# One decoder layer on one core: the 32-row substitution through memory, spatial products in place, q scaled on VectorE

## The chip, the cores and the metric

One Trainium2 chip, one of its cores. The time is device microseconds for one execution of the whole program; the kernel before took 2677.02 us (median of three runs, 2673.93 to 2677.5).

## The reference, cut to what matters

One layer of a hybrid decoder. A group of 2048 new tokens and 8 sample tokens with a stored state share all weights; the width is 1024. One wide input projection feeds branch A (spatial gating in chunks of 128 positions) and branch B (gated DeltaNet with 8 heads of 128, a short convolution on q, k, v); two more projections, merge gates and an output projection follow.

```python
vn = rmsnorm(v, norm_g)
vc = vp.reshape(bsz, n, lc, A_GROUPS, A_GROUP_DIM)
ws = jnp.where(causal, w_s[:, :lc, :lc], 0)
mixed = jnp.einsum('gts,bnsgc->bntgc', ws, vc) + bias
...
t_mat = jnp.where(strict, beta[..., :, None] * kk * decay, 0.0) + jnp.eye(c)
sol = lax.linalg.triangular_solve(t_mat, rhs, left_side=True, lower=True, unit_diagonal=True)
...
q_dec = q * jnp.exp(gc)[..., None]
def step(s, xs):
    v_new = u_c - jnp.einsum('bhck,bhkv->bhcv', w_c, s)
    o_c = jnp.einsum('bhck,bhkv->bhcv', qd_c, s) + jnp.einsum('bhij,bhjv->bhiv', a_c, v_new)
    s = s * gl_c[..., None, None] + jnp.einsum('bhck,bhcv->bhkv', kd_c, v_new)
    return s, o_c
```

The change touches three things of this: the mixing of branch A (`mixed`), the inverse of the unit triangular matrix `t_mat`, and the decay factor on q. The kernel works in chunks of 128.

## The kernel before, in words

**Two halves.** The work is done for f = 0 (1024 tokens) and f = 1 (1032: the other tokens and the 8 samples). In each half a long stream of products runs on TensorE: for every 128 columns of a weight, `products` (line 167) makes 8 x 3 matmuls for each block of tokens, 512 columns wide in the first half and 344 in the second. The three passes are high part by high part, low by high, and high by low of both operands in a rounded type. `load` (line 134) brings a weight block of 512 KB into `raw`, which has one buffer; `split` makes its `hi` on ScalarE (line 147) and its `lo` in two halves on VectorE (line 153), each with two buffers.

**What runs between.** After every STRIDE = 2800 columns of the stream, `step` advances four queues of generators by one `yield` each: the chains (`chq`), the samples (`smq`), the convolutions (`cvq`) and the rest (`bgq`: normalised rows, `v_mix`, then the eight heads in turn). Whatever a generator emits up to its next `yield` is put between the matmuls of the stream at that place; TensorE runs its matmuls in the order written, and the framework orders the other engines' instructions. All DMAs are issued from one queue, SP's, in order.

**v_mix** (line 381) does the mixing of branch A once in each half. `vts` are eight tiles, one for each group, 128 positions by 8 chunks by 128 channels. Each is scaled by the reciprocal norm `rv` on POOL (line 416), multiplied on TensorE by the masked spatial weights `wst` (mx), and VectorE writes `mo` = mx times gain plus bias (line 424), which is stored (line 426) in two pieces of 256 KB a group.

**head** (line 431) prepares one of the eight heads. From pk, the products of k with k and q, VectorE makes the strict triangle `M` and the attention `AT` for eight chunks (lines 500, 501). q is scaled by the decay `G` on POOL (line 503). Then the inverse of the unit triangle begins with the four 32x32 blocks on each chunk's diagonal: all 8 x 4 blocks at once, partition 32q+i holding row i of block q. For each of 31 columns VectorE spreads a row to all partitions of its block with a shuffle (`bc`, line 517), multiplies it by a column of `Yc` (line 518) and subtracts (line 519). `Xc` is the transpose of `Yc`. `Y` and `X` get the blocks (ScalarE line 541, POOL line 544), and the matmuls g1, p2, g2 and p3 join the blocks to 64 and to 128.

```python
        for l in range(31):
            bc = sp.tile([P, 8, 32], F32, tag="bc", name="bc", bufs=2)
            nc.vector.stream_shuffle(bc[:, :, l + 1:], Uc[:, :, l + 1:], [l] * 32)
            nc.vector.tensor_tensor(tmp[:, :, l + 1:], bc[:, :, l + 1:], Yc[:, :, l:l + 1].to_broadcast([P, 8, 31 - l]), ALU.mult)
            nc.vector.tensor_tensor(Yc[:, :, l + 1:], Yc[:, :, l + 1:], tmp[:, :, l + 1:], ALU.subtract)
```

**chain** (line 580) runs the recurrence over a head's eight chunks while the next head is prepared. In each chunk TensorE's p goes to VectorE's r (line 591), r to pz, pz to ScalarE's w (line 597), w to pu, and VectorE's S (line 602) to the next p. After four chunks the output O is normalised (rko, by the helper in lines 93 to 98), scaled (OS, line 614), turned (otr) and written to yT (line 621). **conv** (line 650) makes the short convolution: one product and three product-sums of 128x1024 (line 659) for each of q, k and v of a head.

Tiles with a tag have as many buffers as the tag says; AT has two, the other large tags of a head ("E", "G", "M", "Y", "NV") one.

Of the kernel before, what the change touches and what calls it, by code (L numbers as in the profile page):

```python
# [28 lines left out]
def hybrid_step(tc, d):  # L29
    nc = tc.nc  # L30
    if PIN:
        mm = lambda *a, **k: tc.keep_in_program_order(nc.tensor.matmul(*a, **k))  # L32
# [26 lines left out]
    idc = cst[:, 4 * P + 16:4 * P + 48]  # L59
# [231 lines left out]
    def btile(tag, dt=F32, shape=(P, 8, P)):  # L291
        return sp.tile(list(shape), dt, tag=tag, name=tag, bufs=2 if tag == "AT" else 1)
# [89 lines left out]
    def v_mix(f, vts, ssv, sv):  # L382
# [27 lines left out]
        for g in range(8):  # L410
            wst = sp.tile([P, P], F32, tag="r", name="wst", bufs=2)
            dma(wst, d["ws"][g])
            nc.gpsimd.affine_select(wst, wst, [[1, P]], ALU.is_ge, 0.0, base=0, channel_multiplier=-1)
            bb = sp.tile([P, P], F32, tag="w", name="bb", bufs=2)
            dma(bb, d["bs"][g:g + 1, :].partition_broadcast(P))
            nc.gpsimd.tensor_tensor(vts[g], vts[g], rv.unsqueeze(2).to_broadcast([P, 8, P]), ALU.mult)
            for _ in range(7 if g == 0 else 1):
                yield
            for gi in range(2):
                mx = pg.tile([P, 512], F32, tag="o" if gi == 0 else "kq", name="mx")  # L420
                for n in range(4):
                    mm(mx[:, n * P:(n + 1) * P], vts[g][:, gi * 4 + n, :], wst, start=True, stop=True)
                mo = sp.tile([P, 512], F32, tag="yT", name="mo", bufs=2)
                nc.vector.scalar_tensor_tensor(mo.rearrange("p (n t) -> p n t", t=P), mx.rearrange("p (n t) -> p n t", t=P), gmlpg[:, g:g + 1],
                                               bb.unsqueeze(1).to_broadcast([P, 4, P]), ALU.mult, ALU.add)
                dma(m_sp[f][g][:, gi * 512:(gi + 1) * 512], mo)
                yield


    def head(f, h, T):  # L430
# [84 lines left out]
        for l in range(31):
            bc = sp.tile([P, 8, 32], F32, tag="bc", name="bc", bufs=2)
            nc.vector.stream_shuffle(bc[:, :, l + 1:], Uc[:, :, l + 1:], [l] * 32)  # L517
            nc.vector.tensor_tensor(tmp[:, :, l + 1:], bc[:, :, l + 1:], Yc[:, :, l:l + 1].to_broadcast([P, 8, 31 - l]), ALU.mult)  # L518
            nc.vector.tensor_tensor(Yc[:, :, l + 1:], Yc[:, :, l + 1:], tmp[:, :, l + 1:], ALU.subtract)  # L519
            if (l + 1) * 28 // 31 > l * 28 // 31:  # L520
                yield
        Xc = btile("Xc", shape=(P, 8, 32))
# [9 lines left out]
        NV = btile("NV")  # L532
        for gi in range(2):
            tr = turned(T["v"], "tr", gi)
            for n in range(4):
                c = gi * 4 + n
                nc.scalar.activation(NV[:, c, :], tr[:, tk(n)], AF.Copy, scale=nk[:, c:c + 1])
            if gi == 0:
                for q in range(4):
                    r = slice(32 * q, 32 * q + 32)  # L540
                    nc.scalar.activation(Y[r, :, r], Yc[r], AF.Copy)
                for q in range(2):
                    r = slice(32 * q, 32 * q + 32)
                    nc.gpsimd.tensor_copy(X[r, :, r], Xc[r])
            yield
        g1 = {a: pg.tile([P, 8, 32], F32, tag=t, name="g1") for a, t in ((0, "kq"), (64, "tr"))}
# [15 lines left out]
        nc.gpsimd.tensor_copy(X[32:64, :, 0:32], yt)  # L562
# [170 lines left out]
    def samples():  # L733
# [61 lines left out]
        for h in range(NH):  # L795
# [88 lines left out]
    def v_phase(A, vt_tile, st):  # L884
        spans = [(0, 1), (1, 2), (2, 4), (4, 6), (6, 8)]
        tags = [("Y", 1), ("NV", 1), ("KD", 2), ("KD", 2), ("craw", 2), ("craw", 2), ("AT", 2), ("vT", 1)]
# [31 lines left out]
        def begin():  # L918
# [347 lines left out]
```

## Time and profile before

| | |
|---|---|
| runs | 2677.5, 2673.93, 2677.02 us; median 2677.02 |
| profiled execution | 2677.51 us, span of the trace 2675.7 us |
| mean granted TensorE clock | 0.991 |
| TensorE busy | 2592.4 us, 97% |
| VectorE, ScalarE, POOL busy | 1552.0, 1048.0, 416.5 us |
| moved by DMA | 280.38 MB, mean 105 GB/s |

The span runs from the first to the last instruction of the trace; the profiled execution has 1.8 us around it. Busy times say how full an engine is, not who holds up whom: for that one looks at what an engine waited for. A released wait is written X <- Y: X could begin when Y had ended. In the page's rows a group of instructions has its line, its engine, what it writes and reads, its count, and then busy time and the mean duration of one in ns.

### The profile page before, as it was taken

The page shows a single profiled execution, that of the slowest core. Times are in us where ns is not written, and L with a number is a line of the kernel's source. Part 1 is how long each engine was busy: PE and PEld are TensorE (multiplying, and loading weights), DVE is VectorE, ACT ScalarE, POOL GpSimd, SP SyncE. Part 2 cuts the span into 40 slices and gives each one's busy share as a digit, 9 for nine tenths or more (in the row PEclk, how much of TensorE's full clock was granted, in tenths as well). Part 3 has the DMA queues.
Part 4 walks back from the last instruction along what each step waited for, and adds up shares of the span by engine and source line. Part 5 has one row for each costly group of instructions (what it writes and reads, how often), then busy time and mean ns, then how long its engine had stood idle before and what let it go on. Part 6 is the DMA issues. An engine that isn't in the chain of part 4 may idle for free.

```text
span 2675.7 us, 42486 instructions
## 1 busy us (share of the span) xinstructions
PE 2592.4 (97%) x15755; PEld 2306.2 (86%) x15755; DVE 1552.0 (58%) x5018; ACT 1048.0 (39%) x2732; POOL 416.5 (16%) x536
## 2 busy tenths in 40 slices
PE   7989999999999999999999999999999999999998
PEld 6778787877878888989999999999989888999886
DVE  6266766765865725256677568467484543442455
ACT  5324453453453423423534534435442332332122
POOL 2021121121211102022111212211111102102000
PEclk9989999999999999999999999999999999999999
DMA  6232212211212214123122121121145876645443
GB/s 207 80 118 68 68 40 75 87 44 60 72 48 72 87 64 131 41 69 119 56 62 64 49 84 57 44 77 61 60 123 185 274 243 238 236 170 182 135 141 102
DMA packets 139792, 280.38 MB, mean 105 GB/s; under 512 B 19944, under 2 KB 75688, under 8 KB 139584
## 3 DMA queue, kind: packets, MB, share of 16 engines
q1 hardware_dynamic: 139584, 277.66, 31.7%
q8 instruction: 124, 2.03, 0.3%
q14 instruction: 84, 0.69, 0.1%
HBM read 205.06 MB, written 72.55 MB: 104 GB/s over the span
## 4 chain that ended last, share of the span: by engine, by line
PE 81%; DVE 11%; DMA 4%; ACT 2%; issue 1%; POOL 0%; SPq 0%; ACTq 0%; DVEq 0%; POOLq 0%
PE acc L167 67%; PE acc L947 2%; PE p L32 2%; PE O L32 2%; DVE vT L659 2%; PE trn L33 2%; DMA xt<-in_x_tok 1%; PE pu L32 1%; PE g L32 1%; PE pz L32 1%; PE pk L32 1%; DVE lo L153 1%; DVE bc L517 1%; DMA m<-mo 1%; DVE nwt L96 1%
## 5 line engine op out<-in xcount | busy, mean ns | idle before, releaser
L167 PE MATMUL acc<-Ah,hi 128*128 128x344 f32 (+1 forms) x3360 | 1200.8, 357 | 2.9 <-ACT Ah L209 2.9
L167 PE MATMUL acc<-Al,hi 128*128 128x344 f32 (+1 forms) x3360 | 1197.5, 356 | 0.4
L167 PE MATMUL acc<-Ah,lo 128*128 128x344 f32 (+1 forms) x3344 | 1193.5, 357 | 0.3 <-DVE lo L153 0.3
L167 PEld LDWEIGHTS acc<-Ah,hi 128*128 128x128 f32 x3360 | 634.6, 189 | 59.6 <-ACT Ah L209 4.1
L167 PEld LDWEIGHTS acc<-Al,hi 128*128 128x128 f32 x3360 | 634.8, 189 | 57.1 <-DVE Al L210 1.0
L167 PEld LDWEIGHTS acc<-Ah,lo 128*128 128x128 f32 x3344 | 633.3, 189 | 55.5 <-issue 0.7
L153 DVE TENSOR_TENSOR lo<-raw,hi 128x512 fp32r<-128x512 f32 x368 | 265.2, 741 | 314.3 <-ACT hi L147 301.8
L147 ACT ACTIVATE hi<-raw 128x1024 fp32r<-128x1024 f32 x185 | 195.6, 1057 | 316.9 <-PE acc L167 283.9
L519 DVE TENSOR_TENSOR Yc<-Yc,tmp 128x248 f32<-128x248 f32 (+30 forms) x496 | 149.0, 300 | 10.0
L517 DVE STREAM_SHUFFLE bc<-Uc 128x248 f32<-128x248 f32 (+30 forms) x496 | 151.5, 310 | 0.0
L518 DVE TENSOR_TENSOR tmp<-bc,Yc 128x248 f32<-128x248 f32 (+30 forms) x496 | 146.0, 294 | 0.5
L487 POOL TENSOR_TENSOR kl<-kq,kh 128x256 fp32r<-128x256 f32 x128 | 99.2, 784 | 237.2 <-ACT kh L486 237.0
L659 DVE SCALAR_TENSOR_TENSOR kq<-craw,convw,kq 128x1024 f32<-128x1024 f32 x96 | 122.8, 1279 | 1.2
L591 DVE SCALAR_TENSOR_TENSOR r<-p,neg,NV 128x128 f32<-128x128 f32 x128 | 44.3, 346 | 129.8 <-PE p L32 129.4
L597 ACT ACTIVATE w<-pz,s_bb 128x128 f32<-128x128 f32 x128 | 47.0, 368 | 174.6 <-PE pz L32 174.3
L167 PE MATMUL acc<-Bh,hi 128*128 128x344 f32 (+1 forms) x320 | 111.9, 350 | 0.0
L167 PE MATMUL acc<-Bh,lo 128*128 128x344 f32 (+1 forms) x320 | 111.9, 350 | 0.0
L167 PE MATMUL acc<-Bl,hi 128*128 128x344 f32 (+1 forms) x320 | 111.6, 349 | 0.0
L1115 POOL TENSOR_TENSOR g<-g,u 128x344 f32<-128x344 f32 (+1 forms) x40 | 45.1, 1128 | 337.3 <-DVE g L1114 337.3
L643 ACT ACTIVATE craw<-acc 128x344 f32<-128x344 f32 (+1 forms) x120 | 61.2, 510 | 92.9 <-PE acc L167 92.5
L452 ACT ACTIVATE junk<-trn 128x128 f32<-128x128 f32 x256 | 67.7, 284 | 42.1 <-PE trn L33 42.1
L1114 DVE TENSOR_TENSOR g<-g,acc 128x344 f32<-128x344 f32 (+1 forms) x40 | 23.3, 582 | 100.4 <-PE acc L167 82.3
(333 smaller groups left out, 3448.3 us busy)
## 6 DMA issues: line engine op xcount, KB each, us to landing
raw<-in_w_blk SPq DMA_DIRECT2D x136, 512.0 KB, 3.7
g<-big SPq DMA_DIRECT2D x16, 516.0 KB, 2.9
g<-g SPq DMA_DIRECT2D x16, 516.0 KB, 5.1
xt<-in_x_tok SPq DMA_DIRECT2D x16, 512.0 KB, 4.7
m<-mo SPq DMA_DIRECT2D x32, 256.0 KB, 2.7
G<-gc SPq DMA_DIRECT2D x16, 512.0 KB, 8.9
g<-big SPq DMA_DIRECT2D x16, 512.0 KB, 2.9
yb<-yT SPq DMA_DIRECT2D x32, 256.0 KB, 2.3
```

The lines of the kernel that those rows point to most:

```text
L32: mm = lambda *a, **k: tc.keep_in_program_order(nc.tensor.matmul(*a, **k))
L33: transpose = lambda *a, **k: tc.keep_in_program_order(nc.tensor.transpose(*a, **k))
L147: nc.scalar.activation(j.hi[:, :, :m], j.raw[:, :, :m], AF.Copy)
L153: nc.vector.tensor_tensor(j.lo[:, p, :m], j.raw[:, p, :m], j.hi[:, p, :m].bitcast(F32), ALU.subtract)
L167: nc.tensor.matmul(out, wt[:, k, :m], at[:, k, off:off + w], start=(i == 0), stop=(i == len(passes) * KB - 1))
L452: nc.scalar.activation(junk, tr[:, tk(n)], AF.Square, accum_out=acc[:, c:c + 1])
L487: nc.gpsimd.tensor_tensor(kl, kq[:, :, tk(c)], kh.bitcast(F32), ALU.subtract)
L517: nc.vector.stream_shuffle(bc[:, :, l + 1:], Uc[:, :, l + 1:], [l] * 32)
L518: nc.vector.tensor_tensor(tmp[:, :, l + 1:], bc[:, :, l + 1:], Yc[:, :, l:l + 1].to_broadcast([P, 8, 31 - l]), ALU.mult)
L519: nc.vector.tensor_tensor(Yc[:, :, l + 1:], Yc[:, :, l + 1:], tmp[:, :, l + 1:], ALU.subtract)
L643: nc.scalar.activation(raw[:, 3 + off:3 + off + w], ps[:, :w], AF.Copy)
L659: nc.vector.scalar_tensor_tensor(acc, raw[:, i:i + HALF], convw[:, blk, i:i + 1], acc, ALU.mult, ALU.add)
```

## The change

1. **v_mix.** The scaling goes from POOL to ScalarE, eight activations of 128x128 for each group, written in place. VectorE writes its product over the scaled input instead of into `mo`, and one store of 512 KB replaces two of 256 KB. `wst` and the bias are fetched two groups ahead, and the scaling of group g+1 is issued behind the first mx of group g.
2. **Substitution.** The 32 rows of a block are spread differently: four blocks q of eight chunks n are 32 blocks; a group of four partitions holds one block, and partition g of it every fourth row. `M`'s diagonal blocks are written to memory (`u_sp`, four DMAs) and read back four times, so that each partition has a whole block (`UB`). Then a column needs no shuffle: two VectorE operations on k x w elements with k = l//4 + 1 and w = 31 - l. The result `YB` goes to memory (`y_sp`, one DMA) and comes back in the old layout as `Yc` in 16 DMAs, in pieces of 128 bytes. The start value is a constant `idy`.
3. **q** is scaled by `G` on VectorE in place of POOL. The copies into `X` go from POOL to ScalarE.
4. **Order.** `Xc` and the copies into `Y` and `X` come later, three yields after the turned v; the generators have new yields. "Y" and "NV" get a second buffer, and the head waits for the end of the previous chain but one (`len(chq) > 1`) and for its own v. `UB` uses the tag "E", so the samples' work, which takes that tag after the last head, may begin only after the last substitution. A memory reserve of POOL is set to 1024 bytes.

```diff
-        for g in range(8):
+        def fetch(g):
             wst = sp.tile([P, P], F32, tag="r", name="wst", bufs=2)
             dma(wst, d["ws"][g])
-            nc.gpsimd.affine_select(wst, wst, [[1, P]], ALU.is_ge, 0.0, base=0, channel_multiplier=-1)
             bb = sp.tile([P, P], F32, tag="w", name="bb", bufs=2)
             dma(bb, d["bs"][g:g + 1, :].partition_broadcast(P))
-            nc.gpsimd.tensor_tensor(vts[g], vts[g], rv.unsqueeze(2).to_broadcast([P, 8, P]), ALU.mult)
-            for _ in range(7 if g == 0 else 1):
+            return wst, bb
+
+        def scaled(g, wst):
+            nc.gpsimd.affine_select(wst, wst, [[1, P]], ALU.is_ge, 0.0, base=0, channel_multiplier=-1)
+            for n in range(8):
+                nc.scalar.activation(vts[g][:, n, :], vts[g][:, n, :], AF.Copy, scale=rv[:, n:n + 1])
+
+        ahead = [fetch(0), fetch(1)]
+        for _ in range(4):
+            yield
+        scaled(0, ahead[0][0])
+        for _ in range(3):
+            yield
+        for g in range(8):
+            wst, bb = ahead.pop(0)
+            for gi in range(2):
+                part = vts[g][:, gi * 4:gi * 4 + 4, :]
+                mx = pg.tile([P, 4, P], F32, tag="o" if gi == 0 else "kq", name="mx")
+                for n in range(4):
+                    mm(mx[:, n, :], part[:, n, :], wst, start=True, stop=True)
+                if gi == 0 and g < 7:
+                    scaled(g + 1, ahead[0][0])
+                nc.vector.scalar_tensor_tensor(part, mx, gmlpg[:, g:g + 1], bb.unsqueeze(1).to_broadcast([P, 4, P]), ALU.mult, ALU.add)
                 yield
...
+            dma(m_sp[f][g][:, 0:HALF], vts[g].rearrange("p n t -> p (n t)"))
+            if g < 6:
+                ahead.append(fetch(g + 2))
+            yield
...
-        nc.gpsimd.tensor_tensor(qT, qT, flat(G), ALU.mult)
+        nc.vector.tensor_tensor(qT, qT, flat(G), ALU.mult)
+        yield from wait(1)
+        for q in range(4):
+            r = slice(32 * q, 32 * q + 32)
+            dma(u_sp[f][h][q].rearrange("n i c -> i n c"), M[r, :, r])
+        UB = sp.tile([P, 32, 32], F32, tag="E", name="UB")
+        yield from wait(1)
+        for q in range(4):
+            dma(UB[32 * q:32 * q + 32], u_sp[f][h].rearrange("q n i c -> (q n) i c"))
+        YB = btile("Uc", shape=(P, 8, 32))
+        nc.scalar.activation(YB, idy, AF.Copy)
+        tmp = btile("tmp", shape=(P, 8, 32))
+        yield from wait(4)
+        for l in range(31):
+            k, w = l // 4 + 1, 31 - l
+            nc.vector.tensor_tensor(tmp[:, :k, l + 1:], YB[:, :k, l:l + 1].to_broadcast([P, k, w]), UB[:, l:l + 1, l + 1:].to_broadcast([P, k, w]), ALU.mult)
+            nc.vector.tensor_tensor(YB[:, :k, l + 1:], YB[:, :k, l + 1:], tmp[:, :k, l + 1:], ALU.subtract)
+            if l % 3 == 3 - 1:
+                yield
...
+        dma(y_sp[f][h].rearrange("g q n k c -> (g q n) k c"), YB)
         Yc = btile("Yc", shape=(P, 8, 32))
+        yield
         for q in range(4):
...
+            for g in range(4):
+                dma(Yc[32 * q + g:32 * q + 32:4], y_sp[f][h][g, q].rearrange("n k c -> k n c"))
+        while len(chq) > 1 or not T.get("v_made"):
+            yield
+        Y, NV = btile("Y"), btile("NV")
...
+        yield from wait(3)
+        Xc = btile("Xc", shape=(P, 8, 32))
+        nc.vector.transpose(Xc, Yc)
```

Three places show what moves. The first is VectorE in the first half, where the substitution of a head meets the chain of the head before it (r and S; `Uc` is the tag in which the new `YB` lies). Before:

```order
625 L591 SCALAR_TENSOR_TENSOR r<-p_3768,neg,NV 128x128
626 L518 TENSOR_TENSOR tmp<-bc,Yc 128x8x28
627 L517 STREAM_SHUFFLE bc<-Uc 128x8x27
628 L519 TENSOR_TENSOR Yc<-Yc,tmp 128x8x28
629 L153 TENSOR_TENSOR lo<-raw,hi 128x512
630 L518 TENSOR_TENSOR tmp<-bc,Yc 128x8x27
631 L517 STREAM_SHUFFLE bc<-Uc 128x8x26
632 L519 TENSOR_TENSOR Yc<-Yc,tmp 128x8x27
633 L517 STREAM_SHUFFLE bc<-Uc 128x8x25
634 L518 TENSOR_TENSOR tmp<-bc,Yc 128x8x26
635 L602 SCALAR_TENSOR_TENSOR S<-S,s_eg,pu 128x128
```

The chain's r and S stand between a substitution's columns. And of the kernel changed, the same place, VectorE:

```order
565 L634 SCALAR_TENSOR_TENSOR S<-S,s_eg,pu 128x128
566 L623 SCALAR_TENSOR_TENSOR r<-p_3725,neg,NV 128x128
567 L634 SCALAR_TENSOR_TENSOR S<-S,s_eg,pu 128x128
568 L623 SCALAR_TENSOR_TENSOR r<-p_3754,neg,NV 128x128
569 L153 TENSOR_TENSOR lo<-raw,hi 128x512 x2
570 L634 SCALAR_TENSOR_TENSOR S<-S,s_eg,pu 128x128
571 L542 TENSOR_TENSOR tmp<-Uc,UB 128x31
572 L543 TENSOR_TENSOR Uc<-Uc,tmp 128x31
573 L542 TENSOR_TENSOR tmp<-Uc,UB 128x30
574 L543 TENSOR_TENSOR Uc<-Uc,tmp 128x30
```

The chain's last S now stands ahead of the first column; the shuffles are gone, and a column's two operations begin with 31 elements on each partition.

The second place is VectorE ahead of a head's g1, in the kernel changed: `Xc`, `yt` and what stands around them.

```order
488 L688 TENSOR_SCALAR kq<-craw,convw 128x1024
489 L153 TENSOR_TENSOR lo<-raw,hi 128x512
490 L691 SCALAR_TENSOR_TENSOR kq<-craw,convw,kq 128x1024 x3
491 L623 SCALAR_TENSOR_TENSOR r<-p_3231,neg,NV 128x128
492 L570 STREAM_TRANSPOSE Xc<-Yc 128x256
493 L688 TENSOR_SCALAR kq<-craw,convw 128x1024
494 L691 SCALAR_TENSOR_TENSOR kq<-craw,convw,kq 128x1024 x2
495 L593 STREAM_TRANSPOSE yt<-Y 32x256
```

`Xc` stood directly behind the substitution's last column before; it now stands among the convolution's operations and one r of the chain.

The third is SP's queue in the kernel changed, from the weight loads during a substitution to those behind it.

```order
69 L135 DMA raw<-in_w_blk 128x1024 x3
70 L549 DMA y_0_185<-Uc 128x256
71 L554 DMA Yc<-y_0_185 8x8x32 x16
72 L135 DMA raw<-in_w_blk 128x1024 x2
73 L719 DMA big<-m_1_90 128x1024
```

The store of the result and its sixteen reads stand between weight loads, where only weight loads stood before.

## Rows read from the trace of the kernel before

**Rows 1.** The page: busy time by engine; costliest groups (busy us, mean ns).

```profile
PE 2592.4 (97%) x15755; PEld 2306.2 (86%) x15755; DVE 1552.0 (58%) x5018; ACT 1048.0 (39%) x2732; POOL 416.5 (16%) x536
...
L517 DVE STREAM_SHUFFLE bc<-Uc 128x248 f32<-128x248 f32 (+30 forms) x496 | 151.5, 310 | 0.0
L518 DVE TENSOR_TENSOR tmp<-bc,Yc 128x248 f32<-128x248 f32 (+30 forms) x496 | 146.0, 294 | 0.5
```

**Rows 2.** PE's waits: line, released by, us in total, times, longest.

```profile
PE pz L32 <- DVE r L591: 13.0, 10, 2.9
PE mx L32 <- DVE mo L424: 10.7, 4, 6.6
...
PE p L32 <- DVE S L602: 9.7, 8, 2.1
PE mx L32 <- DVE rx L98: 8.5, 1, 8.5
PE pk L32 <- DVE yT L621: 3.6, 4, 1.1
```

**Rows 3.** Timeline, 134 to 153 us: start, duration, engine, line, operation.

```profile
134.23 1.90 POOL L416 TENSOR_TENSOR AT<-AT,rv 128x1024 f32<-128x1024 f32 x1
134.33 1.82 DVE L93 TENSOR_SCALAR nwt<-ssx 128x9 int32<-128x9 int32 x1
...
134.60 1.05 PE L32 MATMUL mx<-wst,E 128*128 128x128 f32 x8
...
143.60 0.17 DVE L96 TENSOR_TENSOR nwt<-rx 128x9 f32<-128x9 f32 x1
...
146.70 2.04 PE L32 MATMUL mx<-wst,G 128*128 128x128 f32 x8 [8.47 <-DVE rx L98]
...
150.67 1.73 PE L32 MATMUL mx<-wst,G 128*128 128x128 f32 x8
```

**Rows 4.** Busy us (x instructions) of PE, PEld, DVE, ACT, POOL; PEclk; DMA; GB/s.

```profile
134.00:152.00 18.00, 9.53 (x43) 8.10 (x42) 17.66 (x21) 2.72 (x4) 10.67 (x9) 0.72 0.13 37
...
1165.00:1192.00 27.00, 20.36 (x129) 20.10 (x128) 24.84 (x36) 5.08 (x8) 15.37 (x11) 0.90 0.16 46
```

**Rows 5.** Timeline, 400 to 407 us, in which a substitution begins.

```profile
400.92 0.40 PE L167 MATMUL acc<-Ah,lo 128*128 128x512 f32 x1
...
401.15 0.40 PE L167 MATMUL acc<-Ah,hi 128*128 128x512 f32 x1
...
401.71 0.40 DVE L518 TENSOR_TENSOR tmp<-bc,Yc 128x248 f32<-128x248 f32 x1
...
402.15 0.42 DVE L519 TENSOR_TENSOR Yc<-Yc,tmp 128x248 f32<-128x248 f32 x1
...
406.02 0.49 PE L32 MATMUL pz<-r,Y 128*128 128x128 f32 x2 [2.40 <-DVE r L591]
```

**Rows 6.** Groups by line and shape on VectorE and ScalarE.

```profile
L659 DVE SCALAR_TENSOR_TENSOR kq<-craw,convw,kq 128x1024 f32<-128x1024 f32 x96 | 122.8, 1279 | 1.2
...
L518 DVE TENSOR_TENSOR tmp<-bc,Yc 128x48 f32<-128x48 f32 x16 | 3.3, 206 | 0.0
...
L537 ACT ACTIVATE NV<-trn,s_nk 128x128 f32<-128x128 f32 x128 | 36.5, 369 | 36.8 <-PE trn L33 36.7
```

**Rows 7.** DMA issues: count, KB each, median us from issue to landing.

```profile
m<-mo SPq DMA_DIRECT2D x32, 256.0 KB, 2.7
...
Ss<-in_st_gdn SPq DMA_DIRECT2D x16, 512.0 KB, 4.2
...
wst<-in_ws SPq DMA_DIRECT2D x16, 64.0 KB, 4.0
...
m<-ms SPq DMA_DIRECT2D x8, 4.0 KB, 1.5
```

**Rows 8.** Lines 147 and 135, 300 to 330 us: count, duration, first and last.

```profile
L147 ACT ACTIVATE hi<-raw x2: 1062/1065/1068, 305.3 to 323.3; 128x1024 fp32r<-128x1024 f32 x2
...
L135 SPq DMA_DIRECT2D raw<-in_w_blk x2: 332/332/333, 313.3 to 327.2; - x2
...
DMA to landing us min/median/max: 3.7/3.7/3.7
```

More of the change, by code (lines that the diff above doesn't have):

```diff
@@ L291, in btile @@
     def btile(tag, dt=F32, shape=(P, 8, P)):
-        return sp.tile(list(shape), dt, tag=tag, name=tag, bufs=2 if tag == "AT" else 1)
+        return sp.tile(list(shape), dt, tag=tag, name=tag, bufs=2 if tag in ("AT", "Y", "NV") else 1)
     BT = ["E", "G", "M", "AT", "Y", "NV"]
@@ L409, in v_mix @@
             yield
-        for g in range(8):
+        def fetch(g):
             wst = sp.tile([P, P], F32, tag="r", name="wst", bufs=2)
             dma(wst, d["ws"][g])
-            nc.gpsimd.affine_select(wst, wst, [[1, P]], ALU.is_ge, 0.0, base=0, channel_multiplier=-1)
             bb = sp.tile([P, P], F32, tag="w", name="bb", bufs=2)
             dma(bb, d["bs"][g:g + 1, :].partition_broadcast(P))
-            nc.gpsimd.tensor_tensor(vts[g], vts[g], rv.unsqueeze(2).to_broadcast([P, 8, P]), ALU.mult)
-            for _ in range(7 if g == 0 else 1):
-                yield
[L419 to L427, printed above, removed]
@@ L430, in head, with wait @@
+    u_sp = [[dp.tile([4, 8, 32, 32], F32, name=f"u{f}_{h}") for h in range(NH)] for f in range(2)]
+    y_sp = [[dp.tile([4, 4, 8, 8, 32], F32, name=f"y{f}_{h}") for h in range(NH)] for f in range(2)]
+    def wait(n):
+        for _ in range(n):
+            yield
     def head(f, h, T):
@@ L515, in head @@
[L515 to L522, printed above, removed]
@@ L531, in head @@
         nc.gpsimd.memset(X, 0.0)
-        NV = btile("NV")
         for gi in range(2):
@@ L537, in head @@
                 nc.scalar.activation(NV[:, c, :], tr[:, tk(n)], AF.Copy, scale=nk[:, c:c + 1])
[L538 to L544, printed above, removed]
-            yield
+            yield
+        yield from wait(3)
+        Xc = btile("Xc", shape=(P, 8, 32))
+        nc.vector.transpose(Xc, Yc)
+        for q in range(4):
+            r = slice(32 * q, 32 * q + 32)
+            nc.scalar.activation(Y[r, :, r], Yc[r], AF.Copy)
+        for q in range(2):
+            r = slice(32 * q, 32 * q + 32)
+            nc.scalar.activation(X[r, :, r], Xc[r], AF.Copy)
+        yield from wait(2)
         g1 = {a: pg.tile([P, 8, 32], F32, tag=t, name="g1") for a, t in ((0, "kq"), (64, "tr"))}
@@ L661, in conv @@
             nc.scalar.activation(acc, acc, AF.Silu)
+            if kind == 2:
+                T["v_made"] = True
             if after:
@@ L885, in v_phase @@
         spans = [(0, 1), (1, 2), (2, 4), (4, 6), (6, 8)]
-        tags = [("Y", 1), ("NV", 1), ("KD", 2), ("KD", 2), ("craw", 2), ("craw", 2), ("AT", 2), ("vT", 1)]
+        tags = [("Y", 2), ("NV", 2), ("KD", 2), ("KD", 2), ("craw", 2), ("craw", 2), ("AT", 2), ("vT", 1)]
         def x_tile(i):
@@ L933, in begin @@
             dma(convw, d["convw"])
+            dma(idy, d["idy"])
             dma(abraw, d["w_ab"])
@@ L1229 @@
         np.where(idx[:, None] <= idx[None, :], f4(0), f4(-1e30)).astype(f4),
-        fold, np.tile(np.eye(32, dtype=f4), (4, 1)),
+        fold,
     ], axis=1)
```

22 lines of the change are left out of this document (7 added, 15 removed).

## The prediction, made before any run of the changed kernel

> **What bounds the kernel now.** I read the busy table first: TensorE (PE) is busy 2592.4 of 2675.7 us, VectorE 1552.0, POOL 416.5 [rows 1]. So only what lets PE stand or slows its clock can change the time, and its idle sum is 2675.7 − 2592.4 = 83 us. The list of PE's waits says who owns it [rows 2]: the largest end on VectorE results, pz<-r 13.0 us in 10 waits, mx<-mo 10.7 in 4, p<-S 9.7 in 8, mx<-rx 8.5 in one, pk<-yT 3.6 in 4, 45.5 in all. The other 37.5 are the start of the program and many short gaps.
>
> Then I looked where these waits lie. **The stall in v_mix** is one place. From 134 us POOL runs the 128x1024 scalings of L416, 1.90 us each, and VectorE's tiny 128x9 operations between them take 1.82 us each; as soon as POOL is through, the same kind takes 0.17 [rows 3]. PE stands 8.47 us, since a matmul mx waits behind these operations. [...] The second half has the same pattern, weaker, at 1165 to 1192 us, with a clock of 0.90 [rows 4].
>
> **The start of a substitution** is the other place. At 401.71 us VectorE begins a product of 0.40 us, at 402.15 a difference of 0.42 [rows 5], and a shuffle goes with each pair; the chain's r of the head before lies behind several of them, and PE waits 2.40 us at pz until 406.02 [rows 5].
>
> **Gains.** (1) In v_mix the 16 scalings of 1.90 us on POOL become 128 on ScalarE, 128x128 in place. The nearest row, 128x128 with a scale, is 0.37 us [rows 6], 2.95 us a group. Without POOL's long operations VectorE's small ones fall to the 0.17 us of rows 3, and mx<-mo and mx<-rx go: 10.7 + 8.5 = 19.2 us [rows 2]. Some of mx<-mo is a wait for the store that still reads mo, which lands in 2.7 us [rows 7]; in-place writes take it away too. With the stall goes half clock: (2.04 − 1.05) + (1.73 − 1.05) = 1.7 us on mx alone, L167 between them besides, and at most (1 − 0.90) × 27 = 2.7 in the second half. I take 4 for both.
>
> (2) The substitution loses its 496 shuffles and most of its elements. Before, (151.5 + 2 × 146.0)/16 = 28 us of VectorE a head, taking L519 like L518 [rows 1]. After, 62 operations of 50 elements on average; a 128x48 row is 206 ns [rows 6]. I add 34 ns for the dependence of each on the one before (0.44 from the start of the product to that of the difference, for a duration of 0.40 [rows 5]): 62 × 0.24 = 15 us. A first column takes two operations of 0.2 instead of three of 0.4, and in the built order the chain's r and S stand ahead of the substitution (the first place above). So I take 11 of the 13.0 us of pz<-r, and the 3.6 of pk<-yT, since yT stood in the same crowd [rows 2].
>
> [...]
>
> Sum of gains: 19.2 + 4 + 11 + 3.6 = 37.8 us.
>
> **Costs.** (3) The way through memory must end before g1. By rows: u 4 × 0.33 of issue [rows 8] and a landing of 2.7 (m<-mo); UB 4 × 0.33 + 4.2 (512 KB, Ss); substitution 15 and some four lo in it, 3; y 0.3 + 2.7; Yc 16 × 0.33 + 4.0 (wst, the slowest small one) [rows 7]; Xc about 0.4, like the other 256-element operations: 40 us. In the built order 183 to 207 matmuls of L167 stand on PE between a head's last pk and its first g1 in the first half; at 0.23 us (400.92 to 401.15 [rows 5]) 42 to 48 us, and in the second half 264 to 298 of 344 columns, as much. With the chain's matmuls between I take 47: some 7 us of slack, so nothing for the way itself. But Xc stands behind convolution operations of 1.28 us on VectorE [rows 6] (the second place above), and g1 behind it. Bounds: 0, and two such operations each time, 2.56 × 16 = 41. Nearest is p<-S, which also stands behind them and cost 9.7 in all [rows 2]: half of it, 5.
>
> (4) The q scaling on VectorE. No row has a product of two 128x1024 tensors there; with an addition in it, it is 1.28 us [rows 6], so the 16 cost 0 to 20 us. They stand in front of an M or an S now and then; pk alternates between two PSUM tags. I take 2, against a POOL that is freed.
>
> (5) SP's queue gets 25 more issues a head. It is in order: 16 Yc wait for y to land and hold the weight loads behind them (the third place), 2.7 + 16 × 0.33 = 8 us. The cover: a load issued at 313.3 landed 3.7 us later, and its hi began at 323.3, when the block before had ended, 6 us after; and hi is itself made a block of 18 us ahead of its use (305.3 and 323.3) [rows 8]. So nothing. If that cover were gone, 8 × 16 = 128.
>
> (6) ScalarE has to scale a group, 2.95 us, within three steps. A step is 2800 columns, 5.5 matmuls, 1.3 us, and two of the three carry an mx of 1.05 [rows 3]: 6 us, but a hi of 1.06 [rows 8] and copies can stand ahead. Bounds 0 and 2 × 14 = 28; I take 2.
>
> (7) The samples' work, which waits for the last substitution, comes nearer to the half's boundary: 0 to a landing of 4.2 [rows 7]; I take 1.
>
> Costs: 5 + 2 + 2 + 1 = 10. Net −27.8 against the profiled 2677.51 us (span 2675.7, 1.8 around it), which is the highest of the three runs, 0.5 above their median 2677.02: **2650 us**.
>
> **Rivals.** *A: VectorE stays as crowded at the wrong moments.* 62 short operations, a q scaling and Xc put as much in front of r, S and M as now, and only v_mix pays: 19.2 + 4 − 10 = 13, 2664 us. For it: p<-S comes from convolutions, which stay. Against it: at 401 us it is the columns of the substitution that r waits behind.
>
> *B, slower: the way through memory is late at g1.* u and Yc move pieces of 128 bytes. If each of the four landings takes 3 us more than the rows I used (5.7 for 2.7, 7.2 for 4.2), the way is 12 us longer, 5 to 6 beyond the slack, and PE stands 16 × 6 = 96 us: 2650 + 96 = 2746. It decides from 9 us on: 2 beyond the slack, 2 × 16 = 32, eats the gain. Against it: m<-ms landed in 1.5 us [rows 7] in pieces of 32 bytes, though that is only 4 KB. [...]
>
> *C: v_mix's wait only changes hands.* ScalarE, with its hi, copies and silu, is late at each group as POOL was; PE still stands and loses its clock. Then 23.2 comes off the gain: 2673. Against it: in 134 to 152 us ScalarE is busy 2.72 of 18 [rows 4], and six groups of 2.95 fit in.
>
> **Numbers.** Forecast 0.62, A 0.18, B 0.15, C 0.05. The forecast's own range is 2626 to 2673: below, no cost (10), the other 2 of pz, half of p<-S (5) and a fifth of the 37.5 us of short gaps (7); above, costs (3) and (4) at half of their upper bounds, 20 + 10 in place of 7. The range for 8 in 10 reaches over A, C and the shallow end of B: 2626 to 2678. A measurement of this kernel tells a change from none at about 0.2%, 5.4 us. Faster: the forecast 0.62, A 0.15, C 0.02, 0.79 in all. Same: the upper ends of A and C and the shallow end of B, 0.10. Slower: B, 0.11.
>
> **What would show it.** Right: nothing of L416's kind on POOL, the 128x9 operations near 0.17 us throughout, no wait at mx over 1 us, a clock above 0.9 from 134 to 152 us; pz<-r below 3 us; the substitution's operations near 0.2 us. Wrong: a wait of g1 for Xc that recurs in most heads (B, or (3) where it ends on a convolution); p<-S or pk well over 10 us (A, or (4)); mx waiting for a ScalarE scaling (C); acc waiting for hi or lo (5).

## The result, and the profile after

The kernel changed takes 2644.7 us, the median of 2641.1, 2644.7 and 2647.6, against 2677.3 before; the ratio is 0.9873, with a 95% interval of 0.9855 to 0.9891, so 1.3% less. (A fourth execution was a disturbed one of 6500 us, which median and ratio leave out.) The forecast was 2650, with a range of 2626 to 2678. The time is where the sum put it; the experiments show that one term of the sum had the wrong sign and that another was too large.

The profiled execution has a span of 2643.0 us, 32.7 less than before. First its page: the busy line, and the rows of the substitution.

```profile
PE 2589.1 (98%) x15755; PEld 2295.2 (87%) x15755; DVE 1393.2 (53%) x4042; ACT 1085.0 (41%) x2860; POOL 310.1 (12%) x440
...
L542 DVE TENSOR_TENSOR tmp<-Uc,UB 128x60 f32<-128x60 f32 (+24 forms) x496 | 107.7, 217 | 36.9 <-DMA UB<-u 22.5
...
L543 DVE TENSOR_TENSOR Uc<-Uc,tmp 128x60 f32<-128x60 f32 (+24 forms) x496 | 108.1, 218 | 15.2
```

PE is idle for 2643.0 − 2589.1 = 53.9 us, where it was 83.3 [rows 1]: of the 32.7 us, 29.4 are idle time and 3.3 busy time. The substitution is now two operations of 217 and 218 ns where it was three of about 300. The list of PE's waits, in total, times and longest, shows what went and what came.

```profile
PE trn L33 <- DVE KD L484: 5.2, 6, 1.1
PE mx L32 <- POOL wst L418: 4.5, 2, 3.2
PE g L32 <- DVE Xc L570: 4.5, 5, 2.0
PE acc L167 <- ACT Ah L209: 4.0, 3, 1.6
...
PE trn L33 <- DVE yT L653: 1.8, 1, 1.8
PE acc L167 <- ACT hi L147: 1.6, 1, 1.6
PE pk L32 <- DVE yT L653: 1.3, 1, 1.3
...
PE p L32 <- DVE S L634: 0.6, 2, 0.3
...
PE pz L32 <- DVE r L623: 0.4, 1, 0.4
```

Against [rows 2]: pz<-r fell from 13.0 to 0.4, p<-S from 9.7 to 0.6, and mx, which waited 19.2 for VectorE, waits 4.5 for a weight that POOL masks late. New are trn<-KD 5.2 and g<-Xc 4.5. And the same two stretches as in [rows 4], by engine (busy us and instructions of PE, PEld, DVE, ACT, POOL; clock; DMA share; GB/s):

```profile
134.00:152.00 18.00, 18.00 (x104) 15.60 (x103) 11.59 (x24) 17.97 (x52) 1.73 (x4) 1.00 0.39 122
1165.00:1192.00 27.00, 25.67 (x184) 25.38 (x183) 16.86 (x20) 12.04 (x26) 7.47 (x15) 1.00 0.56 177
```

PE is full at full clock where it had 9.53 of 18 us at 0.72. Over the whole span the granted clock is 0.995 where it was 0.991: by that (1 − 0.991) × 2675.7 = 24 us of full clock were lost before and 13 now, an estimate over idle time too; in PE's busy time only the 3.3 us show.

### The profile page after: what moved, and what is told of

Same layout as the page of the kernel before. It is cut to its first block, busy times and chain, and to the rows that moved or that the text cites. A ratio compares the mean times of both kernels' runs of the same rounds, so it can differ in the third digit from the quotient of the medians.

```text
span 2643.0 us, 42188 instructions
## 1 busy us (share of the span) xinstructions
PE 2589.1 (98%) x15755; PEld 2295.2 (87%) x15755; DVE 1393.2 (53%) x4042; ACT 1085.0 (41%) x2860; POOL 310.1 (12%) x440
## 4 chain that ended last, share of the span: by engine, by line
PE 79%; DVE 9%; DMA 4%; SPq 3%; ACT 2%; issue 1%; POOL 0%; DVEq 0%; ACTq 0%; POOLq 0%
PE acc L167 63%; PE acc L982 3%; SPq L554 2%; PE p L32 2%; PE O L32 2%; DVE tmp L542 2%; DMA UB<-u 2%; DVE Uc L543 2%; PE pk L32 1%; DVE kq L691 1%; PE trn L33 1%; PE pu L32 1%; PE g L32 1%; PE pz L32 1%; PE mx L32 1%
## 5 line engine op out<-in xcount | busy, mean ns | idle before, releaser
L542 DVE TENSOR_TENSOR tmp<-Uc,UB 128x60 f32<-128x60 f32 (+24 forms) x496 | 107.7, 217 | 36.9 <-DMA UB<-u 22.5
L543 DVE TENSOR_TENSOR Uc<-Uc,tmp 128x60 f32<-128x60 f32 (+24 forms) x496 | 108.1, 218 | 15.2
L634 DVE SCALAR_TENSOR_TENSOR S<-S,s_eg,pu 128x128 f32<-128x128 f32 x128 | 44.1, 345 | 136.5 <-PE pu L32 135.9
L742 ACT ACTIVATE big<-acc 128x344 f32<-128x344 f32 (+2 forms) x81 | 40.9, 505 | 102.1 <-PE acc L167 101.9
L508 ACT ACTIVATE kh<-kq 128x256 fp32r<-128x256 f32 x128 | 51.9, 416 | 69.2 <-PE pk L32 67.1
```

Of the source, the lines that this page charges most:

```text
L508: nc.scalar.activation(kh, kq[:, :, tk(c)], AF.Copy)
L542: nc.vector.tensor_tensor(tmp[:, :k, l + 1:], YB[:, :k, l:l + 1].to_broadcast([P, k, w]), UB[:, l:l + 1, l + 1:].to_broadcast([P, k, w]), ...
L543: nc.vector.tensor_tensor(YB[:, :k, l + 1:], YB[:, :k, l + 1:], tmp[:, :k, l + 1:], ALU.subtract)
```

## The experiments

All times are medians; "before" was run beside them and gave 2677 us each time. PE's waits, idle time and clock come from the one profiled execution of each.

### v_mix alone

The kernel before with the change's `v_mix` (from `fetch` to the store), nothing else.

```diff
-            nc.gpsimd.tensor_tensor(vts[g], vts[g], rv.unsqueeze(2).to_broadcast([P, 8, P]), ALU.mult)
+            for n in range(8):
+                nc.scalar.activation(vts[g][:, n, :], vts[g][:, n, :], AF.Copy, scale=rv[:, n:n + 1])
...
```

> The kernel before with the new v_mix alone (scaling on ScalarE, in place, fetched two ahead). Theory: the change is two parts that add up. v_mix's waits at mx fall from 19.2 us to about 4.5 (as in the kernel changed, for wst), its slow-clock stretch goes (about 3), everything else stays: 2677 - 18 = 2659 us, 2655 to 2663, with pz<-r and p<-S as before, 20 to 25 us together. Rival: the parts need each other (VectorE must be freed by the shorter substitution before v_mix gains): over 2668.

Measured: 2660.1 us, ratio 0.9938 (0.9923 to 0.9952). pz<-r and p<-S stand at 13.0 and 10.3, and mx waits 2.9. So this part is worth 17 us by itself, as the theory had it; the rival is out.

### Everything but v_mix

The kernel changed with the old `v_mix`, POOL scaling and `mo` tile.

> The kernel changed with the old v_mix. Theory: mx waits are back at 15 to 20 us, the 128x9 operations at 1.8 us; pz<-r and p<-S stay under 3 us together: 2645 + 18 = 2663 us, 2658 to 2667. Rival 1, the substitution part is worth nothing by itself: 2675 or more. Rival 2, v_mix is worth nothing by itself: 2649 or less.

Measured: 2653.9 us, ratio 0.9914 (0.9900 to 0.9929), 23 less than before and only 9 more than the kernel changed, below the theory's range and above the second rival's. mx waits 15.8 again and pz<-r does not appear. Both parts are worth something alone, but 17 + 23 = 40 is more than the 33 of both: they do not add up, and no run shows why.

### POOL's scaling brought back

The kernel changed, with the scaling on POOL and all else of the new v_mix kept: in place, one group ahead, early fetches.

```diff
-            for n in range(8):
-                nc.scalar.activation(vts[g][:, n, :], vts[g][:, n, :], AF.Copy, scale=rv[:, n:n + 1])
+            nc.gpsimd.tensor_tensor(vts[g], vts[g], rv.unsqueeze(2).to_broadcast([P, 8, P]), ALU.mult)
```

> The kernel changed with one thing undone: the groups are scaled on POOL again, one operation of 128x1024 each, still in place, one group ahead, with the new fetches. Theory (what hurt was POOL's long operations beside VectorE's): the 128x9 operations beside a scaling take 1.8 us again and one mx wait of 3 us or more comes back in the first half: 2651 to 2660 us. Rival (what hurt was the mo tile, its store and the late weights): no such wait, at most 2648.

Measured: 2660.5 us, ratio 0.9942 (0.9928 to 0.9957). Its waits of PE, and VectorE's 128x9 operations in its timeline (start, duration):

```profile
PE mx L32 <- DVE rx L98: 8.0, 1, 8.0
PE mx L32 <- DVE E L436: 6.5, 1, 6.5
```

```profile
136.04 1.82 DVE L93 TENSOR_SCALAR nwt<-ssx 128x9 int32<-128x9 int32 x1
...
145.68 0.17 DVE L97 SCALAR_TENSOR_TENSOR nwt<-nwt,ssx 128x9 f32<-128x9 f32 x1
```

The operations are at 1.82 us again beside POOL's and at 0.17 behind them, and two waits of 8.0 and 6.5 us are back at mx. The time is 16 us over the kernel changed, 0.5 beyond the theory's range and more than the 9 that the whole old `v_mix` costs there, which stays open. In-place writes and early fetches don't prevent that: what v_mix gains comes from taking POOL's long operations away from VectorE's small ones.

### q back on POOL, three times

The prediction gave q's move to VectorE a cost of 2 us. Three kernels ask it: the kernel changed with q on POOL again, the kernel before with q on VectorE and nothing else, and the kernel changed with the old v_mix and q on POOL. The edit of the first and the third; the second has it the other way round:

```diff
-        nc.vector.tensor_tensor(qT, qT, flat(G), ALU.mult)
+        nc.gpsimd.tensor_tensor(qT, qT, flat(G), ALU.mult)
```

> The kernel changed with q scaled on POOL again (16 operations of 128x1024, some 2.6 us each). Theory (POOL's long operations slow VectorE's small ones): the 128x4 operations of rko that fall beside one take about 2 us each, and waits of 1 to 2 us come at otr, trn or pk: 2646 to 2655 us. Rival (what the prediction took: the q scaling costs VectorE a little in front of M and S, so undoing it gives that back): 2641 to 2645 us, with pk and p<-S waits shorter.

Measured: 2664.2 us, ratio 0.9947 (0.9931 to 0.9962). That is 19.5 more than the kernel changed, beyond both theories' bounds, on the first one's side. (The profiled execution, 2655.7 us, is the fastest of the six, so its waits show less than the median lost.)

> The kernel before with q scaled on VectorE, nothing else. Theory (POOL's long product slows what VectorE does beside it, whatever the substitution is): the small operations of rko near it fall to 0.16 us, and 5 to 12 us go: 2665 to 2672 us. Rival 1 (it matters only beside the new order, where undoing it cost 19 us): 2674 to 2680. Rival 2 (the prediction's term: 16 operations of 1.2 us more in front of M and S): 2679 or more.

Measured: 2663.7 us, ratio 0.9945 (0.9930 to 0.9960), 1.3 below the theory's range. This one line takes 14 us off the kernel before: p<-S falls from 9.7 [rows 2] to 2.2, pz<-r to 10.1.

```profile
PE pz L32 <- DVE r L591: 10.1, 8, 2.8
...
PE p L32 <- DVE S L602: 2.2, 2, 1.5
```

> The kernel changed with the old v_mix and with q scaled on POOL: what is left of the change is the substitution, its new order and the copies into X on ScalarE. If q's place costs the same with either v_mix (19 us with the new one): 2653.9 + 19 = 2673 us, 2668 to 2677, so that the substitution by itself is worth no more than 4. Rival (the 19 us come from the meeting of q's product with the new v_mix or are the planner's order there): 2655 to 2663.

Measured: 2687.8 us, ratio 1.0035 (1.0022 to 1.0048). Neither: the new substitution with its order, without the moves of v_mix and q, is 10 us slower than the kernel before.

The reason can be read in two places. In the timeline of the kernel before, at a head's last pk, which the prediction had not looked at:

```profile
1631.59 2.73 POOL L503 TENSOR_TENSOR kq<-kq,G 128x1024 f32<-128x1024 f32 x1
...
1632.24 3.15 DVE L659 SCALAR_TENSOR_TENSOR vT<-craw,convw,vT 128x1024 f32<-128x1024 f32 x1
...
1638.61 0.34 DVE L602 SCALAR_TENSOR_TENSOR S<-S,s_eg,pu 128x128 f32<-128x128 f32 x1
...
1639.00 0.49 PE L32 MATMUL p<-S,kq 128*128 128x128 f32 x2 [1.93 <-DVE S L602]
```

While POOL scales q, one of v's convolution operations takes 3.15 us; S and, behind it, p come late, and PE waits 1.93 us. The groups say the same of all 48: line 659, the same operation on the same shape, has a mean of 1279 ns for q and k [rows 6] and 1612 ns for v, where q's scaling falls. In the kernel changed v's has this:

```profile
L691 DVE SCALAR_TENSOR_TENSOR vT<-craw,convw,vT 128x1024 f32<-128x1024 f32 x48 | 61.3, 1277 | 10.4 <-ACT vT L686 9.8
L527 DVE TENSOR_TENSOR kq<-kq,G 128x1024 f32<-128x1024 f32 x16 | 19.5, 1218 | 3.6 <-POOL kl L509 3.6
```

The runs that move q and nothing else say that q's scaling is the cause: v's mean falls to 1328 ns in the kernel before with q on VectorE, and rises to 1645 in the kernel changed with q on POOL.

```profile
L659 DVE SCALAR_TENSOR_TENSOR vT<-craw,convw,vT 128x1024 f32<-128x1024 f32 x48 | 63.7, 1328 | 1.3 <-ACT vT L654 1.1
L691 DVE SCALAR_TENSOR_TENSOR vT<-craw,convw,vT 128x1024 f32<-128x1024 f32 x48 | 79.0, 1645 | 10.3 <-ACT vT L686 9.8
```

So v's convolution alone lost (1612 − 1328) × 48 = 14 us to it before, and lost them where S and M wait: five of the eight p<-S waits of the kernel before, 7.1 of the 9.7 us, come within 5 us behind such a scaling. In all VectorE is busy for less when it scales q itself, 1540.4 us against 1552.0 [rows 1], though the scaling takes 19.5 of them. The second place is the way through memory. With q on POOL and the old v_mix, the timeline at a head's end of pk:

```profile
692.17 3.48 POOL L512 TENSOR_TENSOR kq<-kq,G 128x1024 f32<-128x1024 f32 x1
...
693.58 0.34 DVE L507 SCALAR_TENSOR_TENSOR M<-pk,s_bb,E 128x128 f32<-128x128 f32 x1
...
694.03 2.70 DVE L676 SCALAR_TENSOR_TENSOR vT<-craw,convw,vT 128x1024 f32<-128x1024 f32 x1
...
695.67 0.38 SPq L445 DMA_DIRECT2D G<-gc  x1
...
696.15 3.05 SPq L516 DMA_DIRECT2D u<-M  x4
```

The last M is done at 693.9, but u's first issue is at 696.15 and the four take 3.05 us. Ahead of u in SP's queue stands the load of the next G, which may overwrite the old one only when q has been scaled by it: it is issued at 695.67, 0.03 us after POOL's end. In 4 of 16 heads u begins 2.1 us or more behind M, each time behind such a load, issued 0.02 or 0.03 us after POOL's end; in 3 others its four issues take 3.5 to 6.6 us, for a reason that no run shows. With q on VectorE and the same old v_mix u begins at once in 15 of 16, and no four take over 2.9. The five waits at g1 of 0.7 to 3.6 us lie in heads of these seven, and g1<-Xc is 11.0 us where it was 3.7. PE's idle time, 82.8 us, is then no better than before, and the clock is worse (0.988).

Which of VectorE's operations POOL's held up, the traces show one by one. v's convolution took 2.70 and 3.15 us beside q's scaling, and 1277 ns in the mean of the kernel changed, where VectorE scales q. The 128x9 operations of v_mix took 1.82 beside a scaling and 0.17 without one, also those that read one tensor and a constant (L93: 1.82 at 134.33 us in the kernel before, 0.17 at 136.75 in the kernel changed). M, which reads pk, kept its 0.34 us in the midst of POOL's operation (693.58 us in the timeline above). What sets the two kinds apart no run here shows. How long the wait was, the traces show too: it lasted until POOL was through. In the kernel before eight of v's convolution operations began while POOL scaled q, and each ended 1.07 to 1.09 us after POOL did; the first 128x9 operation of [rows 3] ended 0.02 us after (136.15 against 136.13). Where a convolution operation had begun just before, at 895.02 us for one, it took 1.31 us and POOL's scaling 3.27, in place of the 2.42 that it took at 213.59 us with only M and AT beside it.

### Place or length of the substitution

pz<-r is gone: because r and S now stand ahead of the substitution, or because its operations are short? Two kernels. The first has the old substitution of three long operations a column, without memory, with r and S nearly all outside; the second the new one with 38 r and S between its columns.

```diff
-        yield from wait(4)
+        yield from wait(1)
         for l in range(31):
...
+            nc.vector.stream_shuffle(bc[:, :, l + 1:], Uc[:, :, l + 1:], [l] * 32)
+            nc.vector.tensor_tensor(tmp[:, :, l + 1:], bc[:, :, l + 1:], Yc[:, :, l:l + 1].to_broadcast([P, 8, 31 - l]), ALU.mult)
+            nc.vector.tensor_tensor(Yc[:, :, l + 1:], Yc[:, :, l + 1:], tmp[:, :, l + 1:], ALU.subtract)
```

> The kernel changed, but with the old substitution (three operations a column, no way through memory), begun three steps earlier, so that in the built order only 19 of the chain's r and S stand inside a substitution, in two of the sixteen heads (88 in the kernel before, 7 in the kernel changed). Theory (the place rules): pz<-r and p<-S stay under 6 us together, and lie in the heads with r and S inside; g1 waits for Xc no more; 2640 to 2652 us. Rival (the length of the operations rules): these two waits are back at 15 us or more, spread over the heads; 2658 or more.

Measured: 2692.8 us, ratio 1.0054 (1.0038 to 1.0071), and its waits and one stretch of 14 us (columns as above):

```profile
PE g L32 <- DVE Xc L564: 35.5, 15, 3.4
...
PE pz L32 <- DVE r L617: 3.3, 4, 1.6
...
PE p L32 <- DVE S L628: 1.5, 1, 1.5
```

```profile
690.00:731.00 41.00, 41.00 (x194) 33.40 (x193) 37.31 (x140) 17.44 (x39) 8.33 (x9) 1.00 0.28 84
731.00:745.00 14.00, 10.57 (x103) 7.50 (x102) 4.66 (x23) 5.27 (x13) 0.40 (x1) 0.76 0.21 75
```

pz and p wait 4.8 us together, as the theory of the place had it, and in the heads with r and S inside. But the time is far beyond both forecasts, for something neither had: g1 waits in 15 heads, up to 3.4 us each. In the first half, its first head apart, g1 stands 128 to 147 matmuls behind the last pk in the built order, not 183 to 207: the framework, which by these counts also sets the order of the matmuls (not the order written alone, as the description ahead has it), lets g1 follow, as it seems, when it takes Xc for done. I call it the planner below. And such a wait cost more than itself here: the 14 us around one, in which PE stands 3.4 us, have a clock of 0.76, after 41 us at 1.00 in which PE was always busy. 35.5 us of g1 waits go with (0.995 − 0.982) × 2695 = 35 us of lost clock, of which 25 show in PE's busy time (2614.3 us against 2589.1).

> The kernel changed, with the substitution begun eight steps later, so that 38 of the chain's r and S stand between its columns instead of 7 (88 in the kernel before). Theory 1 (the place rules): waits at pz and p come back, 8 us or more together, 2653 us or more. Theory 2 (a column of two short operations is too short to hold r or S up): pz<-r and p<-S stay under 4 us together; what is lost then is at g1 only, 2640 to 2655.

 (`wait(4)` ahead of the first column became `wait(12)`.)

Measured: 2637.2 us, ratio 0.9853 (0.9836 to 0.9869); pz<-r 3.2 and p<-S 0.6. The second theory's waits hold, the time is 3 us below its range: a column of two operations, 0.44 us together, didn't hold r up for long. Either the place or the length takes most of pz<-r away (with 38 r and S inside, not 88, in the second kernel); the change has both. This kernel's median is also 7.5 us below that of the kernel changed, but the intervals of the two ratios overlap, so that isn't shown to be a gain.

### The way through memory

Its steps in the first head of the kernel changed, from the timeline of VectorE and SP's queue:

```profile
208.74 0.35 DVE L522 SCALAR_TENSOR_TENSOR M<-pk,s_bb,E 128x128 f32<-128x128 f32 x1 [0.25 <-PE pk L32]
...
209.12 1.81 SPq L531 DMA_DIRECT2D u<-M  x4
...
216.75 1.71 SPq L535 DMA_DIRECT2D UB<-u  x4
...
221.07 0.19 DVE L542 TENSOR_TENSOR tmp<-Uc,UB 128x31 f32<-128x31 f32 x1 [4.12 <-DMA UB<-u]
...
246.57 0.33 SPq L549 DMA_DIRECT2D y<-Uc  x1
...
248.27 12.35 SPq L554 DMA_DIRECT2D Yc<-y  x16
...
263.58 0.44 DVE L570 STREAM_TRANSPOSE Xc<-Yc 128x256 f32<-128x256 f32 x1
```

From the last M to the end of Xc are 55 us, and 48.5 us as a mean of the 16 heads (45 to 56), where the prediction had 40. The largest step of the difference is the sixteen reads of Yc: they take 12.35 us of issue here and 11.4 in the mean, 0.71 each, where a weight load takes 0.33 [rows 8] and 5.3 us were taken. The next is the way from UB's last issue to the first column, 6.5 us in the mean where 4.2 was taken. This head, the second longest, is slow in two other steps that don't hold for all: its 62 operations take 25.5 us with what VectorE does between them (221.07 to 246.57), and UB begins only 5.8 us after u's last issue (210.9 to 216.75); the means are 18.2 and 3.3 us, near the 18 and 2.7 that were taken.

To see what a longer way costs, each read of Yc was issued twice (`dma` of line 554, twice in a row).

> The kernel changed with each of the sixteen reads of Yc issued twice in a row: 16 more issues of 0.66 us a head, 10.5 us on the way through memory and in SP's queue. Theory 1 (the slack of 6 to 7 us that the prediction worked out): g1 waits some 4 us longer in each head, 64 us, so 2700 to 2720 us. Theory 2 (hardly any slack is left, as 5 of 16 heads wait already): 8 to 10 us in nearly each head, 130 to 160 us, and PE at a lower clock behind them, 2780 us or more. Rival (the reads overlap and Xc waits for something else): 2655 or less.

Measured: 2771.7 us, ratio 1.0354 (1.0315 to 1.0392), between the theories; there were two executions, 2782.2 and 2761.3, and the slower is the profiled one. Its busy line and waits:

```profile
PE 2664.2 (96%) x15755; PEld 2344.8 (84%) x15755; DVE 1391.3 (50%) x4042; ACT 1085.9 (39%) x2860; POOL 304.2 (11%) x440
```

```profile
PE g L32 <- DVE Xc L571: 44.8, 12, 6.4
PE p L32 <- ACT tmp L585: 14.0, 18, 2.8
...
PE acc L167 <- ACT hi L147: 8.7, 10, 2.4
```

The planner saw the reads and moved g1 some 50 matmuls back, 12 us in the first half and 8 in the second; the way became 13.6 us longer, and g1 waits 44.8 us, what follows it 14.0, and the weights, which stand behind the reads in SP's queue, 8.7 in 10 places (one of them, 1.6 us, behind the last head). The larger part is the clock: PE is busy 75 us longer with the same work, at 0.964, and idle 62 us longer.

Then the way was made shorter: rows in order in memory, so that one store in small pieces and four reads of 1 KB rows do.

```diff
-        dma(y_sp[f][h].rearrange("g q n k c -> (g q n) k c"), YB)
+        dma(y_sp[f][h].rearrange("k g q n c -> (g q n) k c"), YB)
...
-            for g in range(4):
-                dma(Yc[32 * q + g:32 * q + 32:4], y_sp[f][h][g, q].rearrange("n k c -> k n c"))
+            dma(Yc[32 * q:32 * q + 32], y_sp[f][h][:, :, q].rearrange("k g n c -> (k g) n c"))
```

> The kernel changed with another layout of the substitution's result in memory: rows in order, so that one store in pieces of 128 bytes and 4 reads in pieces of 1 KB take the place of one store in pieces of 1 KB and 16 reads in pieces of 128 bytes. Theory (the 16 issues of 0.66 us and the pieces make the way through memory long): Yc is there 7 us or more earlier after the last column, g1<-Xc goes from 4.5 us to under 1, 2637 to 2643 us. Rival (the store in small pieces costs what the reads save, or Xc waits for the convolution on VectorE): g1<-Xc stays at 3 us or more, 2644 or more.

Measured: 2664.3 us, ratio 0.9959 (0.9946 to 0.9972): 20 slower than the kernel changed, with g1<-Xc at 18.3, the rival's figures for another reason. The store and the reads are quick: y lands in 2.3 us and Yc's parts in 1.7. The way is 38.9 us, 9.6 shorter. But the planner counts on that too and puts g1 142 to 161 matmuls behind pk (first half, first head apart), earlier by 9.9 us in the mean of all heads: no room is gained, and single heads lie further off, with a g1 wait of up to 5.4 us. What decides here is not the length of the way but where the planner puts g1 against it.

### Weights with three buffers, and the way with room

The wait that v_mix kept, in the timeline of the kernel changed:

```profile
153.96 1.05 PE L32 MATMUL mx<-wst,AT 128*128 128x128 f32 x8
...
155.08 0.33 SPq L412 DMA_DIRECT2D wst<-in_ws  x1
...
160.06 0.65 POOL L418 TENSOR_SCALAR_AFFINE_SELECT wst<-wst 128x128 f32<-128x128 f32 x1 [5.67 <-DMA wst<-in_ws]
...
160.77 2.08 PE L32 MATMUL mx<-wst,Y 128*128 128x128 f32 x8 [3.21 <-POOL wst L418]
```

SP issues the next weight only when the group two before it has been multiplied (155.0); it lands, POOL masks it at 160.06, and PE has waited 3.21 us. So three buffers:

```diff
-            wst = sp.tile([P, P], F32, tag="r", name="wst", bufs=2)
+            wst = sp.tile([P, P], F32, tag="wst", name="wst", bufs=3)
...
-        ahead = [fetch(0), fetch(1)]
+        ahead = [fetch(0), fetch(1), fetch(2)]
```

> The kernel changed with spatial weights and biases fetched three groups ahead, in tags of their own with three buffers (SP issues a weight load only when the group two before has been multiplied). Theory: mx<-wst falls from 4.5 us to under 1, and the slow clock behind it goes: 2637 to 2641 us. Rival (the loads are late for SP's queue, not for the buffer): mx<-wst stays at 3 us or more, 2643 to 2648.

Measured: 2632.3 us, ratio 0.9832 (0.9816 to 0.9848), 5 us below the theory's range: no wait at mx any more, and a clock of 0.997. It is 12 us faster than the kernel changed. Last, this together with the rows in order, and five yields more ahead of Xc (`wait(3)` became `wait(8)`):

> Three buffers for the spatial weights (2632 us alone), the result's rows in order (one store, four reads), and five more steps ahead of Xc, since with fewer reads the order had put g1 earlier, 142 to 161 matmuls behind pk instead of 183 to 207, and PE waited 18 us there; it is 169 or 170 now. Theory (the way through memory really is 7 us shorter, the planner had only taken 9): g1<-Xc under 4 us, 2626 to 2633 us. Rival (the small pieces of the store take what the reads gave): g1<-Xc 8 us or more, 2645 or more.

Measured: 2617.8 us, ratio 0.9776 (0.9761 to 0.9790), better than expected and the best of all; its busy line and its waits at g1:

```profile
PE 2570.4 (98%) x15755; PEld 2294.5 (88%) x15755; DVE 1381.7 (53%) x4042; ACT 1084.3 (41%) x2860; POOL 308.0 (12%) x440
```

```profile
PE g L32 <- DVE Xc L569: 2.5, 3, 1.7
```

Apart from its waits g1 would begin 4.3 us behind the end of Xc in the mean of the heads, where it was 0.2 us in the kernel changed and 0.3 us ahead of Xc with the rows in order alone: now there is room. PE is idle for 45.9 us and busy 19 us less than in the kernel changed. Part of that is the clock (0.997 against 0.995, 5 us); the rest wasn't taken apart, nor what the five yields would give without the rows in order.

## Why the prediction was right, and where it was wrong

The runs with v_mix, substitution (with its order and the copies into X) and q, each old or new, in us:

| | q on POOL | q on VectorE |
|---|---|---|
| v_mix old, substitution old | 2677 | 2664 |
| v_mix new, substitution old | 2660 | not run |
| v_mix old, substitution new | 2688 | 2654 |
| v_mix new, substitution new | 2664 | 2645 |

**(1) v_mix: right, a little too large.** 21 us were forecast (19.2 + 4 − 2) and 17 measured alone, 9 on top of everything else. The mechanism is shown by POOL's scaling brought back. What the term missed is that the weights come late, two mx waits of 3.2 and 1.3 us, over the 1 us that the prediction allowed; what it charged for ScalarE (2) didn't come: no mx waits for a scaling. The 4 us for the clock are borne out: the trace of the kernel before has a granted clock of 0.50 from 143.0 to 150.6 us, and with the new v_mix alone the mean clock is 0.995 against 0.991 and PE is busy 4.8 us less (2587.6 against 2592.4).

**(2) The substitution: the waits went, the gain didn't come from there.** pz<-r fell by 12.6 where 11 was taken, and the two operations cost what the row of 206 ns said (217). yT's 3.6 nearly stayed, 1.8 at trn and 1.3 at pk. But the substitution alone, with q where it was, made the kernel 10 us slower, and only with q on VectorE 10 us faster (2664 to 2654). The 14.6 us of this term (11 + 3.6) are not its own.

**(3) The way through memory: the wait was right, the slack was not.** 5 us were taken for Xc behind a convolution and 4.5 measured, in five heads. In three of them Xc does start as a convolution's operation or an r ends, in two as the last read of Yc lands. The way is 48.5 us and not 40, the reads of Yc above all, so the 7 us of slack weren't there but 0.2; the planner had put g1 back just far enough. Rival B's mechanism is real: the reads issued twice cost 127 us, more than its 96, as the clock fell with the waits at g1 (0.964 against 0.995).

**(4) q: the step that failed.** The prediction charged 2 us for 16 operations in front of M and S, "against a POOL that is freed", and took p<-S to come from convolutions, "which stay". They stay, but p<-S waited for the most part because POOL's scaling of q lengthened them: it fell from 9.7 to 2.2 with q alone moved, and to 0.6 in the kernel changed, 9.1 us that no term counted as a gain. The move is worth 14 us in the kernel before, 19.5 in the kernel changed and 34 with the old v_mix. The prediction read what POOL's scalings did to VectorE in v_mix (0.17 to 1.82 us), where it showed as a single large wait, and did not ask where else POOL runs a long operation beside VectorE. The convolution's two means, 1279 and 1612 ns, were the row that told it.

**(5) to (7).** SP's queue cost nothing in any head: the one acc<-hi, 1.6 us, lies at 2099 us, behind the last of them, where hi stands behind other work of ScalarE. That is although an issue of Yc takes 0.66 to 0.77 us where 0.33 was taken. The half's boundary (7) cost some 2 us (pc 1.0, and acc<-Ah 4.0 where it was 2.9); 1 was taken. No term is there for trn<-KD, 5.2 us where it was 0.2; it comes without the new v_mix too (5.4), and why no run shows.

Rivals A and C did not come: pz, p and pk wait some 4 us in all, and mx never for ScalarE. So that the sum came out so near is luck, two errors that cancel: the substitution was credited with some 15 us, and q's move, charged with 2, brought about as much.

## What to carry to other kernels

Look for the same operation on the same shape with two means: here 1279 and 1612 ns pointed to a collision, the timeline showed with which engine, and that engine's operation was worth moving although the busier engine then did it itself (2677 to 2664 us). Where a planner sets the order, a part made faster can lose, since what depends on it is put earlier too (here a way 9.6 us shorter and a kernel 20 us slower); look at where the dependent instruction stands in the order, and give it room. And price a wait of TensorE above its length: over 14 us in which it stood 3.4 us the clock was at 0.76.

## What the runs showed that was not expected

- A read of Yc, 8 KB in pieces of 128 bytes, holds SP's queue for 0.66 us (median of 256), a weight load of 512 KB for 0.33.
- Lost clock was of the size of the waits: beside 35.5 us of g1 waits PE was busy 25 us longer, beside 67.5 us (g1, p, acc) 75 longer, both against the kernel changed. Its busy time for the same work went from 2570 us (clock 0.997) to 2664 (clock 0.964).
- POOL's operations of 128x1024 lengthened VectorE's tenfold for the small ones (0.17 to 1.82 us) and by 1.4 to 1.9 us for the large (1.27 to 2.70 and 3.15). The eight convolution operations that began beside one ended 1.07 to 1.09 us behind it, a 128x9 operation 0.02 us behind; M's 0.34 us stayed as they were.
